# Two orders of work in a Hyena and retention block: retention beside the last input products, and beside the output projection

## The chip, the cores and the metric

The kernel runs on one core of a Trainium2 chip. The metric is the device time of one execution in microseconds; the time given is the median of several runs. The engines are PE (TensorE, matrix products), DVE (VectorE), ACT (ScalarE), POOL (GpSimd) and SP, which here only issues DMAs; "SP's queue" is the list of DMA issues that SP works off in program order, one wait after the other.

## The reference

One layer of a block with two kinds of token mixers that read the same projection of the normed and modulated input. T = D = 1024; the Hyena part has 512 channels, the retention part eight heads of 64, in chunks of 128 tokens, run in both directions.

```python
ux = hx @ w_in                                  # x0, x1, v of Hyena; q, k, v, g of retention
x0, x1, v = split(short_conv(u_hyena))
y_hy = bidir_long_conv(v * x1, filters, bias) * x0     # by FFT
q, k = rope(q), rope(k)                         # pairs of neighbouring channels are turned
o = retention(q, k, v, forward) + flip(retention(flipped, backward))
#   per chunk: (q k^T * decay mask) v  +  (q * w_q) state
o = (o - mean) * rsqrt(var + eps) * gn_g        # per head
y_ret = o * silu(g)
x = x + gate * (concat(y_hy, y_ret) @ w_out)
x = x + gate2 * relu(hx2 @ w1)^2 @ w2           # MLP, then a last norm
```

## The kernel before

All large products are made in three matmuls each (`mm3`, L182): an operand is split into a high part of reduced precision and a low rest, and high by high, high by low and low by high are added in PSUM. A weight is brought in as a *slab* of 256 or 512 columns: `slab` (L193) loads it in halves (`wr_...`), ScalarE casts the high part (`wh_...`), VectorE subtracts for the low part (`wl_...`). `prefetch` (L221) asks for the next slab of a fixed list (`order`). `hxh` and `hxl` are the input's two parts, feature by token.

The program is recorded in the order of the Python code and then ordered for each engine by a scheduler; work within `with urgent():` is given priority. What an engine, or a DMA queue, has in its list is worked off in that order.

The work in question runs in three stages.

*Convolution, about 256 to 511 us.* For each half `hv` of the 512 channels: products x1, vh and x0 (`feature_major`, tile `px...`), short convolutions on ScalarE and VectorE (`short_conv`, L818), a transform loop of eight rounds in which PE makes `pXv` (forward) and `pGv` (back) and VectorE multiplies by the filter and adds (`dft_const`, `butterflies`), and the gated result, stored as `mix_d` (tile `vxl`). Products of the next part stand between the rounds: those of x0 of the half, x1 and vh of the next, and in the second loop the gate products g (`pgt`, token by feature, `token_major`, L519). Among them stand the pieces of `modulation` (L686): eight loads of w_ada (`adaw`), eight VectorE operations that add them up (`adac`), four small products (`pada`). There are eight pieces in all; two of them stand in the second transform loop and behind it.

*q, 511 to 555 us.* q is made token by feature as well (`pq`, 384 matmuls of 256 columns; g has as many). `rope` (L551) turns it on VectorE (`qr`, `rpq`) and writes it twice side by side (`q`), so that `q_d` holds each head's 64 channels twice. Then the pools of the input parts are closed, and the places of the output projection opened (`big`, with `place`, L1012).

*Retention and output projection, 555 to 712 us.* The mixed Hyena channels are loaded back (`mraw`) and split into `mx` (`split_mix`, L1036). `retention` (L1059) is called for 16 chunks, eight of heads 0 to 3 and then eight of heads 4 to 7. For one chunk it loads q (`q2l`), k, v and the states (`ktl`, `vtl`, `stl`); PE transposes q of four heads (`pqd`, L1074); VectorE makes `qw` (q times the decay) and ScalarE copies q into tiles with zeros in the other head's rows (`sgqz`); two products of 256 columns make the scores (`psc`, L1083); VectorE multiplies them with the mask (`sT`); 16 small products of 64 columns, two side by side in PE's columns, make the output `po` (L1093); VectorE and ScalarE form mean and square sums (`mu`, `ctrs`, `sqo`, `gss`). After four chunks `group_norm` (L1105) scales, multiplies by silu(g), transposes (`pz`) and writes the two parts `mr`. With every second chunk stands one `out_conv` (L1045), 24 matmuls `poh` of 512 columns that multiply the mixed Hyena channels by half of w_out, added to x (`XN`). After that `out_ret` (L1228) does the same for `mr` (`por`, 192 matmuls), and the MLP follows, which takes the second half of the time.

PSUM: `ps_mm` gives tiles of two banks for the large products; `ps_aux` and `ps_cv` (L176, L179) give single banks, by two tags.

## Time and profile before

| | |
|---|---|
| median of 3 runs | 1372.75 us (1372.7 to 1382.48) |
| profiled execution | 1372.26 us |
| its span | 1370.5 us |
| mean granted PE clock | 0.979 of full |
| PE busy | 1284.9 us, 94% |
| VectorE busy | 964.2 us, 70% |
| ScalarE busy | 524.7 us, 38% |
| DMA traffic | 278.19 MB, mean 203 GB/s |

The profiled execution's own time holds 1.8 us around its span. All rows are of this one execution. A matmul row's duration overlaps with the next one's; the pace is the distance between starts. A time line's row gives the start, the duration, the engine, the line and the operation, and in brackets how long the engine had stood idle and what ended that. The granted clock is a share of full speed: 1.00 is 2.4 GHz, and 0.50 would be 1.2 GHz throughout.

### The profile page before, as it was taken

To read this page: it belongs to the slowest core of one execution; us is meant where nothing else is said; L and a number is where in the kernel's file an instruction comes from. 1 tells how busy PE (TensorE), PEld (TensorE's weight loads), DVE (VectorE), ACT (ScalarE), POOL (GpSimd) and SP (SyncE) were. 2 spreads that over 40 slices of the span, in tenths; PEclk is the share of its full clock that TensorE was granted. 3 is DMA by queue.
4 is the path that set the end of the run, shared out by engine and by line. 5 is a ranking of instruction groups with operands and counts; after the bars stand their busy time and mean duration, and the time that the engine had idled before them with its cause. 6 is when DMAs were issued, how large, how long until landed. Compare 5 with 4: busy or idle time off the path is not lost.

```text
span 1370.5 us, 20044 instructions
## 1 busy us (share of the span) xinstructions
PE 1284.9 (94%) x7374; PEld 1075.9 (79%) x7374; DVE 964.2 (70%) x1709; ACT 524.7 (38%) x903; POOL 19.9 (1%) x24
## 2 busy tenths in 40 slices
PE   6899899999998989799897999999998999999996
PEld 1488788878887989677776888887886888888896
DVE  5798587557788766558887988888656955555563
ACT  6654422222132121223455444444444744344420
POOL 0310000000000000000000000000000000000000
PEclk9899999999999999999998999999999999999999
DMA  9545656465436544875321788988636996666621
GB/s 372 212 154 162 215 177 194 143 204 170 139 133 202 178 155 169 274 241 182 114 87 60 251 299 326 337 311 292 245 123 227 342 321 187 196 200 186 198 79 62
DMA packets 139570, 278.19 MB, mean 203 GB/s; under 512 B 14672, under 2 KB 47056, under 8 KB 137040
## 3 DMA queue, kind: packets, MB, share of 16 engines
q1 hardware_dynamic: 137744, 272.19, 59.4%
q0 software_dynamic: 1152, 4.19, 0.8%
q8 instruction: 58, 0.95, 0.3%
q10 hardware_dynamic: 576, 0.52, 0.1%
q14 instruction: 40, 0.33, 0.1%
HBM read 193.75 MB, written 83.10 MB: 202 GB/s over the span
## 4 chain that ended last, share of the span: by engine, by line
PE 72%; DVE 11%; DMA 9%; ACT 4%; issue 3%; SPq 1%; POOL 0%; DVEq 0%; ACTq 0%; POOLq 0%
PE px L185 6%; PE px L183 5%; PE px L184 5%; PE py L185 5%; PE py L183 5%; PE py L184 5%; PE pw L183 4%; PE pw L185 4%; PE pw L184 4%; DMA dft_f_k<-in_dft_f 1%; PE pGv L886 1%; PE psc L1083 1%; PE pq L185 1%; PE pq L184 1%; PE pq L183 1%
## 5 line engine op out<-in xcount | busy, mean ns | idle before, releaser
L1176 DVE TENSOR_TENSOR mt<-tr,mt 128x512 fp32r<-128x512 f32 x112 | 76.8, 688 | 99.1 <-ACT mt L1175 98.8
L1175 ACT CAST mt<-tr 128x512 fp32r<-128x512 f32 x112 | 69.5, 621 | 123.6 <-PE py L185 65.2
L183 PE MATMUL px<-mt,mw 128*128 128x512 f32 (+1 forms) x320 | 112.0, 350 | 2.9 <-ACT mw L1175 2.3
L184 PE MATMUL px<-mt,mw 128*128 128x512 f32 (+1 forms) x320 | 112.2, 351 | 1.0 <-DVE mt L1176 1.0
L185 PE MATMUL px<-mt,mw 128*128 128x512 f32 (+1 forms) x320 | 111.5, 349 | 0.1
L1176 DVE TENSOR_TENSOR mw<-wr,mw 128x512 fp32r<-128x512 f32 x112 | 76.7, 687 | 4.4 <-ACT mw L1175 4.3
L183 PE MATMUL py<-mt,mw 128*128 128x512 f32 x192 | 74.7, 389 | 0.0
L184 PE MATMUL py<-mt,mw 128*128 128x512 f32 x192 | 74.7, 389 | 0.0
L185 PE MATMUL py<-mt,mw 128*128 128x512 f32 x192 | 74.7, 389 | 0.0
L1175 ACT CAST mw<-wr 128x512 fp32r<-128x512 f32 x112 | 69.0, 617 | 9.3 <-DMA wr<-s_d 4.8
L183 PEld LDWEIGHTS px<-mt,mw 128*128 128x128 f32 x320 | 60.9, 190 | 11.3 <-ACT mw L1175 2.8
L184 PEld LDWEIGHTS px<-mt,mw 128*128 128x128 f32 x320 | 60.9, 190 | 9.3 <-DVE mt L1176 1.3
L185 PEld LDWEIGHTS px<-mt,mw 128*128 128x128 f32 x320 | 60.8, 190 | 8.4 <-DVE mw L1176 0.7
L183 PE MATMUL px<-hxh,wh_x 128*128 128x512 f32 x128 | 50.9, 398 | 0.0
L185 PE MATMUL px<-hxh,wl_x 128*128 128x512 f32 x128 | 50.9, 398 | 0.0
L184 PE MATMUL px<-hxl,wh_x 128*128 128x512 f32 x128 | 50.7, 396 | 0.0
L697 DVE SCALAR_TENSOR_TENSOR adac<-adaw,cs,adac 128x512 f32<-128x512 f32 x56 | 41.9, 748 | 11.2 <-DMA adaw<-in_w_ada 10.4
L185 PE MATMUL pk<-wh_k,hxl 128*128 128x256 f32 x128 | 39.4, 307 | 3.1 <-DVE hxl L423 3.1
L184 PEld LDWEIGHTS py<-mt,mw 128*128 128x128 f32 x192 | 36.0, 188 | 7.5
L183 PEld LDWEIGHTS py<-mt,mw 128*128 128x128 f32 x192 | 36.0, 188 | 7.5
L185 PEld LDWEIGHTS py<-mt,mw 128*128 128x128 f32 x192 | 36.0, 188 | 7.4
L184 PE MATMUL pk<-wl_k,hxh 128*128 128x256 f32 x128 | 38.4, 300 | 0.9 <-DVE wl_k L207 0.9
(491 smaller groups left out, 3731.5 us busy)
## 6 DMA issues: line engine op xcount, KB each, us to landing
tr<-t_d SPq DMA_DIRECT2D x112, 256.0 KB, 4.0
adaw<-in_w_ada SPq DMA_DIRECT2D x64, 256.0 KB, 4.2
WH<-in_w_mlp SPq DMA_DIRECT2D x16, 1024.0 KB, 7.6
s_d<-WH SPq DMA_DIRECT2D x16, 1024.0 KB, 4.8
wr<-s_d SPq DMA_DIRECT2D x64, 256.0 KB, 4.0
wr<-in_w_mlp SPq DMA_DIRECT2D x48, 256.0 KB, 4.2
t_d<-c SPq DMA_DIRECT2D x40, 256.0 KB, 4.0
t_d<-CH SPq DMA_DIRECT2D x40, 256.0 KB, 5.0
```

The source lines that it names most:

```text
L183: PE.matmul(o, lhsT=lh, rhs=rh, start=first, stop=False, **kw)
L184: PE.matmul(o, lhsT=lh, rhs=rl, start=False, stop=False, **kw)
L185: PE.matmul(o, lhsT=ll, rhs=rh, start=False, stop=last, **kw)
L697: V.scalar_tensor_tensor(ac, wa, cs[:, k, 0:1], ac, op0=ALU.mult, op1=ALU.add)
L886: PE.matmul(o, lhsT=y[:, 0, cb], rhs=iv[:, sl[0]], start=True, stop=False)
L1083: PE.matmul(pc[:, pr * 256:(pr + 1) * 256], lhsT=kt[:, pr], rhs=qT[:, 2 * pr:2 * pr + 2].rearrange("p h c -> p (h c)"), start=True, stop=True)
L1175: A.copy(hi, src)
L1176: V.tensor_tensor(lo, src, hi.bitcast(F32), op=ALU.subtract)
```

## The change

*Columns of w_in.* The host reorders q's and k's columns of each head, so that a rope pair's first members stand in the first 32 channels and the second members in the other 32. `rope` (now for k alone) swaps halves instead of neighbours, and the form that writes its result twice is gone. A new constant `ropeT` holds the tables feature by token.

*Slabs.* Loads of the seventh slab and later ones are issued by GpSimd in place of SP. The list has x0's slabs behind x1 and vh of both halves, then q, g of heads 0 to 3 and q, g of heads 4 to 7.

*Convolution.* The loop over `hv` is cut into `conv_in`, `conv_gate`, `conv_dft` and `conv_out`, called in another order; the five modulations here stand after the first input part, after the second, and after the first gate part.

*q and g* are made feature by token. q0 and g0 come after the convolution's code, q1 and g1 in eight parts of 24 matmuls (`last_products`). `rotate` turns q: four DMAs swap the 32-row halves into `qs`, three VectorE operations of 128x1024 follow, and the result goes to `q_d`.

*Retention* loads q already transposed, each chunk twice (`q2`, upper and lower 64 rows). Transposes, zero tiles and copies go; the scores are four products of 64 rows and 128 columns into a `ps_cv` and a `ps_aux` bank; `sT` is made in two halves.

*Heads.* `heads(0)` runs the eight chunks of heads 0 to 3, with two parts of `last_products` ahead and one after each of the first six. The gate is multiplied in together with the norm's weight, and results go to DRAM (`y_d`). Then the pools are exchanged, and `heads(1)` runs the other eight chunks, with one `out_conv` after each; the earlier results are loaded back and split (`split_ret`). A pool `gap` keeps room so that `mx`, `mr00` and `mraw` lie where the first heads' tables do not.

```diff
-            SP.dma_start(raw, src[:, ks])
+            (SP if nxt[0] < 6 else G).dma_start(raw, src[:, ks])
...
+    yy0 = conv_dft(0, conv_in(0))
+    for _ in range(2):
+        modulation()
+    vT1 = conv_in(1)
+    for _ in range(2):
+        modulation()
+    conv_gate(0)
+    modulation()
+    with urgent():
+        conv_out(0, yy0)
+    conv_gate(1)
+    yy1 = conv_dft(1, vT1)
+    with urgent():
+        conv_out(1, yy1)
...
+    def rotate(hh, b, qf):
+
+        qs = scp.tile([P, T], F32, tag="sc", bufs=3, name=f"qs{hh}{b}")
+        for i in range(4):
+            SP.dma_start(qs[32 * i:32 * i + 32], qf[32 * (i ^ 1):32 * (i ^ 1) + 32])
+        V.tensor_tensor(qs, qs, rot[:, 1], op=ALU.mult)
+        V.tensor_tensor(qf, qf, rot[:, 0], op=ALU.mult)
+        V.tensor_tensor(qf, qf, qs, op=ALU.add)
+        SP.dma_start(q_d[hh][b * P:(b + 1) * P], qf)
+
+    def last_products():
+
+        for kind in "qg":
+            wh, wl = slabs.pop((kind, 1))
+            for b in range(2):
+                o = scp.tile([P, T], F32, tag="sc", bufs=3, name=f"{kind}f1{b}")
+                for h in range(2):
+                    ps = ps_cv(f"p{kind}1{b}{h}")
+                    cc = slice(512 * h, 512 * h + 512)
+                    for k in range(KC):
+                        mm3(ps, wh[:, k, b * P:(b + 1) * P], wl[:, k, b * P:(b + 1) * P], hxh[k][:, cc], hxl[k][:, cc],
+                            k == 0, k == KC - 1)
+                    with urgent():
+                        if kind == "q":
+                            A.copy(o[:, cc], ps)
+                            if h:
+                                rotate(1, b, o)
+                        else:
+                            A.activation(o[:, cc], ps, AF.Silu)
+                            SP.dma_start(sg_d[2 + b][:, cc], o[:, cc])
+                    yield
             prefetch()
...
+        q2 = rtl.tile([P, 4, P], F32, tag="q2", bufs=2, name=f"q2l{nm}")
+        for r in range(2):
+            SP.dma_start(q2[64 * r:64 * r + 64], q_d[hh].rearrange("(h d) t -> d h t", h=4)[:, :, n * P:(n + 1) * P])
...
-        pq = ps_aux(f"pqd{nm}")
-        for h in range(4):
-            PE.transpose(pq[:, h * P:(h + 1) * P], q2[:, h], ident)
...
-        pc = ps_aux(f"psc{nm}")
+        pc = ps_cv(f"psc{nm}0"), ps_aux(f"psc{nm}1")
         for pr in range(2):
-            PE.matmul(pc[:, pr * 256:(pr + 1) * 256], lhsT=kt[:, pr],
-                      rhs=qT[:, 2 * pr:2 * pr + 2].rearrange("p h c -> p (h c)"), start=True, stop=True)
+            for s in range(2):
+                rows = slice(64 * s, 64 * s + 64)
+                PE.matmul(pc[s][:, pr * P:(pr + 1) * P], lhsT=kt[rows, pr], rhs=q2[rows, 2 * pr + s],
+                          start=True, stop=True)
...
-        V.tensor_tensor(ctr, ctr, sg, op=ALU.mult)
...
-            hi, lo = mr[g][0][:, blk], mr[g][1][:, blk]
-            A.activation(hi, pt, AF.Copy, scale=gn)
-            V.scalar_tensor_tensor(lo, pt, gn, hi.bitcast(F32), op0=ALU.mult, op1=ALU.subtract)
+            V.scalar_tensor_tensor(sg[:, pr], pt, gn, sg[:, pr], op0=ALU.mult, op1=ALU.mult)
+            if hh == 0:
+                SP.dma_start(y_d[pr][g], sg[:, pr])
+            else:
+                split_ret(g, blk, sg[:, pr])
...
+    for _ in range(2):
+        next(products)
+
+    heads(0, last_heads)
...
+    for k in range(4):
+        split_mix(k)
+    for d in range(KC):
+        SP.dma_start(xn[d], I["xT"][d * P:(d + 1) * P])
...
+    heads(1, projection)
```

On VectorE, at the first chunk of heads 0 to 3, the order is now this; `qs` and `qf` are the two tiles of `rotate` for q1, `wl_g` is a slab's low part.

```order
L212 TENSOR_TENSOR wl_g_4730<-wr_g_4735,wh_g_4729 128x1024
L1012 TENSOR_TENSOR qs_4806<-qs_4806,rot 128x1024
L1013 TENSOR_TENSOR qf_4753<-qf_4753,rot 128x1024
L1084 TENSOR_TENSOR qw_0_4826<-q2l_0_4816,tabq_4751 128x512
L1014 TENSOR_TENSOR qf_4753<-qf_4753,qs_4806 128x1024
L1094 TENSOR_TENSOR sT_0_4834<-psc_00_4828,tabq_4751 128x2x128
L1094 TENSOR_TENSOR sT_0_4834<-psc_01_4829,tabq_4751 128x2x128
```

Before, `qw` and `sT` of the first chunk stood among the low parts of `mx`, behind the rope of the last q products; now rotate's three operations stand ahead of `sT`.

On PE, a late chunk of heads 0 to 3 stood like this before (`po` rows are those of one chunk, the number behind a name tells buffers apart):

```order
L1083 MATMUL psc_7_5902<-sgqz,ktl_7_5886 128x256 x2
L1074 MATMUL pqd_0_5966<-cols,q2l_0_5957 128x128 x4
L183 MATMUL poh_6340<-mx_5398,wh_o_5557 128x512
L184 MATMUL poh_6340<-mx_5399,wh_o_5557 128x512
L185 MATMUL poh_6340<-mx_5398,wl_o_5558 128x512
L1093 MATMUL po_7_5907<-vtl_7_5888,sT_7_5905 64x64 x2
L1093 MATMUL po_7_5907<-stl_7_5890,qw_7_5898 64x64 x2
```

and the second chunk of these heads stands like this now, where `pq` is a matmul of a product part:

```order
L190 MATMUL pq_4861<-hxh_348,wl_q_4616 128x512
L1090 MATMUL psc_10_4899<-q2l_1_4887,ktl_1_4890 128x128
L1090 MATMUL psc_11_4900<-q2l_1_4887,ktl_1_4890 128x128
L1090 MATMUL psc_10_4899<-q2l_1_4887,ktl_1_4890 128x128
L1090 MATMUL psc_11_4900<-q2l_1_4887,ktl_1_4890 128x128
L1090 MATMUL psc_21_4981<-q2l_2_4968,ktl_2_4971 128x128 x2
L1102 MATMUL po_1_4908<-vtl_1_4892,sT_1_4905 64x64 x2
L1102 MATMUL po_1_4908<-stl_1_4894,qw_1_4897 64x64 x2
L188 MATMUL pq_4933<-hxh_341,wh_q_4615 128x512
L1102 MATMUL po_1_4908<-vtl_1_4892,sT_1_4905 64x64 x2
```

The transposes are gone, the scores are single products by turns into two banks with half of the next chunk's behind them, and products no longer stand between scores and `po`.

On SP, where q's products ended and the mixed channels were loaded, the queue before was:

```order
L994 DMA q_d_4391<-q_5239 128x2x512
L994 DMA q_d_4391<-q_5247 128x2x512
L1021 DMA tabq<-tab_d 128x2048
L1040 DMA mraw<-mix_d_2891 128x512
L994 DMA q_d_4391<-q_5352 128x2x512
L1040 DMA mraw<-mix_d_2891 128x512
L1040 DMA mraw<-mix_d_2892 128x512
L205 DMA wr_o_5563<-in_w_out 128x1024
L994 DMA q_d_4391<-q_5360 128x2x512
```

and between the first and the second four heads it is now:

```order
L1224 DMA XN_5425<-in_xT 128x1024 x4
L1129 DMA y_d_1_4490<-sgs_4750 128x512
L1129 DMA y_d_1_4492<-sgs_4750 128x512
L1075 DMA q2l_0_5483<-q_d_4488 64x4x128 x2
L1077 DMA ktl_0_5486<-kT_d_1345 128x256
L1062 DMA tabq<-tab_d 128x2048
L1197 DMA mraw<-mix_d_2891 128x512 x2
L1197 DMA mraw<-mix_d_2892 128x512 x2
```

The loads `mraw<-mix_d` stood behind stores of q; now they stand behind the stores `y_d` of the last group norm of heads 0 to 3, behind q and k of the next chunk and behind a table.

## Rows read from the trace of the kernel before

**Rows 1.** The page: busy us, share of the span, instructions.

```profile
PE 1284.9 (94%) x7374; PEld 1075.9 (79%) x7374; DVE 964.2 (70%) x1709; ACT 524.7 (38%) x903; POOL 19.9 (1%) x24
```

**Rows 2.** Stretches: seconds; busy us (instructions) of five engines; granted PE clock; DMA share; GB/s.

```profile
380.00:405.00 25.00, 25.00 (x115) 20.62 (x114) 20.76 (x38) 7.58 (x11) 0.00 (x0) 1.00 0.31 115
500.00:525.00 25.00, 21.53 (x175) 21.32 (x174) 9.46 (x14) 5.08 (x6) 0.00 (x0) 0.93 0.48 167
525.00:550.00 25.00, 25.00 (x223) 25.00 (x222) 16.45 (x24) 2.11 (x2) 0.00 (x0) 1.00 0.42 153
550.00:575.00 25.00, 17.14 (x86) 13.24 (x85) 13.95 (x21) 7.76 (x12) 0.00 (x0) 0.86 0.77 245
```

**Rows 3.** Time line of PE, one chunk: start, us, instruction, count, [idle before].

```profile
630.91 0.34 PE L1093 MATMUL po<-vtl,sT 128*64 128x64 f32 x4
...
631.99 0.50 PE L185 MATMUL poh<-mx,wl_o 128*128 128x512 f32 x1
...
632.80 1.02 PE L1083 MATMUL psc<-sgqz,ktl 128*128 128x256 f32 x4
633.66 0.60 PE L1074 MATMUL pqd<-cols,q2l 128*128 128x128 f32 x4
634.01 0.47 PE L185 MATMUL poh<-mx,wl_o 128*128 128x512 f32 x1
```

**Rows 4.** Time lines of PE and VectorE, second convolution half.

```profile
441.16 0.67 PE L886 MATMUL pGv<-dft_i_v,yv 128*128 128x256 f32 x2 [3.30 <-issue]
...
502.66 0.75 DVE L697 SCALAR_TENSOR_TENSOR adac<-adaw,cs,adac 128x512 f32<-128x512 f32 x1 [3.75 <-DMA adaw<-in_w_ada]
...
506.15 1.05 PE L700 MATMUL pada<-ones,adac 128*128 128x2 f32 x8 [3.47 <-DVE adac L697]
```

**Rows 5.** Time line of all engines, from q's products to out_conv.

```profile
556.87 0.50 PE L183 MATMUL poh<-mx,wh_o 128*128 128x512 f32 x1 [2.04 <-ACT mx L1042]
557.87 0.37 SPq L994 DMA_DIRECT2D q_d<-q  x1
...
558.28 1.22 SPq L1040 DMA_DIRECT2D mraw<-mix_d  x2
...
559.73 0.77 PE L183 MATMUL poh<-mx,wh_o 128*128 128x512 f32 x1 [2.36 <-DVE rpq L558]
...
562.10 1.21 ACT L1042 CAST mx<-mraw 128x512 fp32r<-128x512 f32 x2 [5.29 <-DMA mraw<-mix_d]
...
562.51 0.80 PE L184 MATMUL poh<-mx,wh_o 128*128 128x512 f32 x1 [2.01 <-DVE mx L1043]
```

**Rows 6.** Time line of PE, a chunk of heads 0 to 3.

```profile
610.91 1.13 PE L1083 MATMUL psc<-sgqz,ktl 128*128 128x256 f32 x4 [1.88 <-ACT sgqz L1080]
```

**Rows 7.** Time line of PE, out_ret.

```profile
678.66 0.80 PE L183 MATMUL por<-mr,o3h 128*128 128x512 f32 x1 [2.79 <-DVE XN L1243]
679.25 0.63 PE L184 MATMUL por<-mr,o3h 128*128 128x512 f32 x1
...
684.80 0.41 PE L185 MATMUL por<-mr,o3l 128*128 128x512 f32 x1
```

**Rows 8.** Groups of VectorE (busy us, mean ns), then time lines: last po, last scaled ctrs.

```profile
L1086 DVE TENSOR_TENSOR sT<-psc,tabq 128x512 f32<-128x512 f32 x16 | 11.0, 689 | 4.1 <-PE psc L1083 3.8
...
L564 DVE TENSOR_TENSOR q<-qr,rpq 128x1024 f32<-128x1024 f32 x2 | 2.4, 1190 | 0.0
...
661.54 0.29 PE L1093 MATMUL po<-stl,qw 128*64 128x64 f32 x4
...
665.13 1.22 DVE L1112 TENSOR_TENSOR ctrs<-ctrs,rso 128x1024 f32<-128x1024 f32 x1
```

**Rows 9.** DMA issues, 500 to 712 us: count, KB each, median us to landing.

```profile
q2l<-q_d SPq DMA_DIRECT2D x16, 256.0 KB, 3.2
XN<-in_xT SPq DMA_DIRECT2D x8, 512.0 KB, 7.4
...
mraw<-mix_d SPq DMA_DIRECT2D x8, 256.0 KB, 5.9
```

More of the change, by code (lines that the diff above doesn't have):

```diff
@@ L824, in short_conv, with conv_in @@
                                op0=ALU.mult, op1=ALU.add)
-    for hv in range(2):
+    def conv_in(hv):
         vT = vtp.tile([P, NCH, 256], F32, tag="vT", name=f"vT{hv}")
-        Gs = cvp.tile([P, 2, 8, 256], F32, tag="Gs", name=f"Gs{hv}")
         x1t = []
@@ L999, in tile_hymba_block, with last_heads @@
+    opool("gap", side="right").tile([P, 4 * 1024], F32, name="gap")
+    open_retention()
+    retention_tables(lambda nm: rt["l" if nm == "tabq" else "p"].tile([P, 4, 512], F32, name=f"{nm}0"))
+    products = last_products()
+    def last_heads(g, j):
+        next(products, None)
+    for _ in range(2):
+        next(products)
+    heads(0, last_heads)
+    cpool("rtp")
+    cpool("rtl")
+    cpool("gap")
     cpool("vtp")
```

284 lines of the change are left out of this document (150 added, 134 removed).

## The prediction

> **What bounds the kernel now.** I read the busy times first: PE works 94% of the span [rows 1], so a microsecond is gained only where PE has less to do, stands idle, or runs at the lower of its two clocks. Next the table of stretches, for those three. The products run at their pace where the clock is granted in full: 115 matmuls of 512 columns in 25 us, 0.217 us each, and 223 of 256 columns in 25 us, 0.112 us each [rows 2]. Twice the second is the first, so products written feature-major (384 of 512 columns in place of 768 of 256) gain nothing. In the stretches of 500 and 550 us PE lacks time and clock (0.93 and 0.86) [rows 2]. Then the time lines there, for what PE waited for. Three places stand out.
>
> - The second convolution half: 3.30 us ahead of a pGv, and 3.47 us ahead of a pada, where VectorE's adac had itself waited 3.75 us for a load of w_ada [rows 4].
> - The step from q's products to the out_conv products: 2.04, 2.36 and 2.01 us [rows 5]. On SP the store of q stands at 557.87, and the mraw loads go out behind it at 558.28; their data are there at 562.10, when ScalarE casts them. A load that needs nothing waited because the store ahead of it in the queue did.
> - The last out_ret products: 2.79 us, then matmuls at 0.427 us (13 steps from 679.25 to 684.80), the lower clock [rows 7].
>
> **What the change removes.** I sum against the profiled execution's 1372.26 us; the median of the runs, 1372.75, is 0.5 above it, and I make nothing of that.
>
> - Transposes: four take 0.35 us (633.66 to 634.01) [rows 3], in 16 chunks: -5.6. The wait of 1.88 us for ScalarE's copy of them [rows 6]: -1.9.
> - Scores: two products took 0.86 us (632.80 to 633.66) [rows 3], recorded as four matmuls of 256 columns, 0.215 each. Now there are four products of 128 columns on half the rows each, taken by turns from the upper and the lower 64 rows into two banks: the same 0.86 if they run one behind the other, 0.43 if pairs run side by side. The trace has no row-split matmul, but po is split by columns: 32 entries of 64 columns in 1.08 us (630.91 to 631.99) [rows 3], 0.034 each, where 64/256 of 0.215 is 0.054, so those pairs gain a factor of 1.6. I take that, 0.54: -5.1, with -6.9 and 0 as bounds.
> - The step at 555 to 572: 6.4 us of waits, and 0.14 of 25 us in clock, 3.5 [rows 2, 5]: -9.9. What is late there instead stands below.
> - out_ret: 2.79, and 5.55 us for 13 matmuls that cost 2.8 at full pace [rows 7]: -5.5. The group norm that made VectorE late there no longer multiplies by the gate in an extra pass, and its products are ready earlier.
> - Convolution: no modulation stands in the second loop now. Its two waits are 6.8 us, and the clock loses 0.07 of 25 us at the one [rows 2, 4], which I assume at the other too: 10.3. The pada wait must go (5.2); the other was for a chain on VectorE in which adac was only a part, so I take -9 in all. Bounds: -10.3, and +3.5 if the modulations, which now stand among the short convolutions and the first loop, bring one such wait more than they take.
>
> Sum: -37.0.
>
> The slab loads from the seventh on, issued by GpSimd, I cost at nothing: each is asked for one product part ahead, some 5 us of PE. If that cover fails, a part waits for the rest of its load: at XN's 7.4 us for as many bytes [rows 9], 2.2, in up to four parts 9. It belongs to the range. rope loses no operation. The changed order of convolution parts keeps products beside every step of the first DFT loop.
>
> **What it adds.** (1) *Ahead of the first scores.* After the second q product part PE has only the scores and then the first po, which needs sT. On VectorE sT stands behind rotate's three operations of 128x1024, the first of which waits for four moves of q's halves, which wait for ScalarE's copy. Copy 0.6 (two casts of 128x512 take 1.21) [rows 5]; the moves, which no row shows, as q2l's 3.2 [rows 9]; three operations at 1.19, as q's add [rows 8], 3.6; qw 0.7 and half of sT 0.35 [rows 8]: 8.4, less the scores' 0.5: 7.9. After such a wait PE ran at half clock [rows 7], which cost 2.7. Together +10.6; bounds 4 (the moves in 2, no clock lost) and 13.
>
> (2) *The chunks of heads 0 to 3.* The scores write two banks that the product parts also use, so a part stands behind po, not between scores and po. Per chunk PE waits for both halves of sT, 0.69 [rows 8], and I add 0.4 for two hand-overs: 1.1, in seven chunks +7.7. Bounds: 0.4 each, where the next scores already ran ahead (3), and 1.9 each, as the wait of this kind [rows 6] (13).
>
> (3) *From the first to the second four heads.* SP's queue has the two y_d stores of the last group norm, then q2l, ktl, tabq and only then the mraw loads, which wait for nothing else; and all out_conv products need mx from mraw. From the last po to the scaled ctrs the same chain takes 661.83 to 666.35, 4.5 us [rows 8]; the transposes (0.9, as many columns as the scores had) and two operations of the size of sT, 1.4: 2.3. Then five issues at some 0.4 (0.37 for a store) [rows 5], 2.0; a mraw load, 3.8 in the first of these rows [rows 5] and 5.9 in the median [rows 9], taken as 4.8; the cast 0.6; and VectorE's lo halves of the first two, as sT, 1.4. That is 15.6, less 1.3 for transposes and scores in between: 14.3, plus the half clock's 2.7: +17.0; bounds 11 and 24.
>
> (4) *Heads 4 to 7.* Five or more out_conv products stand between scores and po, over 1 us, so that (2) doesn't recur; with out_ret +1, bounds 0 and 5.5.
>
> Sum: +36.3. In all 1372.26 - 37.0 + 36.3 = 1371.6.
>
> The trace's price for changing between whole and split use of PE's array is in these rows: po's 1.08 us hold 0.1 us more than its eight groups at 0.12, and that is all a change and the way back can have cost. The Trainium skill (TensorEngine Tiling (Array Packing), Tiling Modes) speaks against the new scores: changing the tiling mode, not just the tile, drains the engine. With two changes more in each chunk at 0.1, 16 chunks would cost 3.2 us, and the sum would be 1374.8.
>
> **The rivals.**
> *The new waits come out at their low ends.* The same places, but the moves land in 2 us, scores run ahead in every chunk, and the clock is given back at once. Then (1) is 4, (2) 3, (3) 14.3 without the clock: -6.6, -4.7, -2.7, and the full convolution gain -1.3: 1356.3. For it: the order of PE has half of the next chunk's scores ahead of some po. Against it: around the long waits of rows 5 and 7 the clock did fall.
> *SP's queue becomes the bound: slower.* The loads of chunks 4 to 7 stand behind sg_d and q stores that wait for product parts, and 4 MB of XN loads (eight) go out just ahead of the y_d stores. XN loads land in 7.4 us, mraw in 5.9 [rows 9]. If loads behind waiting stores take 7.4, they are longer than a product part (24 x 0.217 = 5.2): 2.2 more in each of four chunks, 8.8, and at (3) 2.6 for mraw plus 7.4 for XN in its way, 10: 1390.4. It decides from the point at which such a load takes longer than one part. For it: exactly this queue held mraw before. Against it: the chunks' own loads land in some 3 us [rows 9], well within a part.
> *The row-split scores run one behind the other.* +5.1: 1376.7. For it: no row shows them; against it: po. It lies within the forecast's band.
>
> **How the numbers follow.** The forecast, with the third rival in it, gets 0.44, the first rival 0.32, the slow one 0.24. 1% is 13.7 us, about what a measurement of this kernel can tell from no change: faster is below 1359, slower above 1386.5. The first rival lies beyond the one, the second beyond the other. Terms (1) to (3) are sums of gaps that no row shows; their bounds reach 17 below and 15 above, and with those of scores, convolution and (4) 21 below: 1350. Upward the slow rival lies past them, at 1390. So the range is 1350 to 1390, and the forecast's own, with half of these bounds, 1361 to 1380.
>
> **What would show it.** Right: no pqd; out_ret without a gap; no pada in the second DFT loop and the clock full there; after the second pq part of heads 4 to 7 a wait of about 8 us for sT; about 1 us ahead of po in each early chunk; and one stretch without PE of 12 to 16 us between the last pz of the first heads and the first poh, with mraw issued just behind y_d. Scores of 0.54 per chunk. Wrong: mraw landed before the group norm ended; waits of one kind that recur in each chunk above 2 us; or the convolution no shorter.

## The result, and the profile after

The changed kernel takes 1396.27 us in the median of four runs (1393.23 to 1405.89), beside 1374.64 us of the kernel before in four runs on the same chip: a ratio of 1.0148, with an interval of 1.0113 to 1.0183. It is slower by about 1.5%; 1371.6 was forecast, and the time lies above the range as well. The profiled execution took 1393.23 us with a span of 1391.4, against 1372.26 and 1370.5.

The page's busy line answers to [rows 1]:

```profile
PE 1285.0 (92%) x6990; PEld 1056.5 (76%) x6990; DVE 961.1 (69%) x1707; ACT 520.2 (37%) x881; POOL 30.5 (2%) x44
```

PE is busy for the same 1285 us, in a span that is 20.9 us longer. To see where these went I cut both spans at ends and starts of PE's work that both kernels have: the last `ps` (which ends the first stage), the last `pgt` (half of the q and g products done, the convolution behind it) and the first `py` (the MLP).

| stretch | before | after | difference | forecast |
|---|---|---|---|---|
| start, up to the last `ps` | 255.7 | 262.0 | +6.3 | 0 |
| convolution and half of q and g | 255.6 | 247.9 | -7.7 | -9 |
| rest of q and g, heads, output projection | 200.8 | 222.1 | +21.3 | +8.3 |
| MLP, to PE's last instruction | 652.2 | 652.5 | +0.3 | 0 |

The heads are the place. The stretches of the changed kernel there (columns as in [rows 2]) show two holes:

```profile
500.00:525.00 25.00, 20.96 (x92) 16.88 (x90) 12.41 (x22) 5.58 (x8) 1.06 (x2) 1.00 0.69 227
525.00:550.00 25.00, 15.45 (x115) 12.09 (x116) 9.25 (x16) 1.30 (x3) 0.00 (x0) 0.66 0.64 174
550.00:575.00 25.00, 22.28 (x167) 17.58 (x167) 12.73 (x22) 7.41 (x11) 1.05 (x2) 0.93 0.55 168
575.00:600.00 25.00, 18.65 (x196) 14.98 (x195) 12.48 (x29) 3.81 (x7) 0.53 (x1) 1.00 0.63 203
600.00:625.00 25.00, 8.51 (x33) 6.23 (x34) 9.39 (x16) 5.92 (x9) 0.00 (x0) 0.52 0.73 260
```

Between 600 and 625 us PE works for 8.5 us of 25, at a granted clock of 0.52; between 525 and 550 us it works at 0.66. PE's time line of the changed kernel has these waits:

```profile
531.80 1.22 PE L1090 MATMUL psc<-q2l,ktl 64*128 64x128 f32 x8 [10.85 <-DMA ktl<-kT_d]
535.62 0.48 PE L1102 MATMUL po<-vtl,sT 128*64 128x64 f32 x4 [2.60 <-issue]
...
555.31 0.34 PE L1102 MATMUL po<-vtl,sT 128*64 128x64 f32 x4 [0.50 <-DVE sT L1094]
...
564.97 0.34 PE L1102 MATMUL po<-vtl,sT 128*64 128x64 f32 x4 [2.15 <-issue]
...
607.14 1.97 PE L1124 MATMUL pz<-cols,ctrs 128*128 128x128 f32 x8 [11.08 <-DVE ctrs L1120]
614.52 1.22 PE L1090 MATMUL psc<-q2l,ktl 64*128 64x128 f32 x8 [5.41 <-DMA ktl<-kT_d]
619.68 1.22 PE L188 MATMUL poh<-mx,wh_o 128*128 128x512 f32 x2 [3.93 <-ACT mx L1199]
...
630.79 0.72 PE L1090 MATMUL psc<-q2l,ktl 64*128 64x128 f32 x8
631.44 0.50 PE L190 MATMUL poh<-mx,wl_o 128*128 128x512 f32 x1
...
721.06 0.50 PE L188 MATMUL por<-mr,o3h 128*128 128x512 f32 x1 [0.45 <-DVE XN L1341]
```

The first two rows are the waits ahead of the first scores and of the first `po`, the next two smaller ones in later chunks, and then come three waits in a row at the step to heads 4 to 7. The scores' rows answer to [rows 3]: 0.65 us from their start to that of the next product. The last is all that is left of the gap of out_ret [rows 7].

What PE waited for at the step stands on ScalarE and VectorE. ScalarE first:

```profile
597.08 0.42 ACT L1109 ACTIVATE sqo<-ctrs 128x256 f32<-128x256 f32 x1 [1.39 <-DVE ctrs L1106]
602.35 1.04 ACT L211 CAST wh_o<-wr_o 128x1024 fp32r<-128x1024 f32 x1 [4.84 <-DMA wr_o<-in_w_out]
603.41 1.28 ACT L291 ACT_TABLE_LOAD   x1
604.70 0.22 ACT L291 ACTIVATE rs_yo<-gss 128x16 f32<-128x16 f32 x1
```

The cast of the last half of the last slab stands ahead of the group norm's `rs_yo` and waits 4.84 us for its load, which GpSimd issued at 593.98. VectorE shows the same order, with `wl_o` ahead of the norm:

```profile
597.99 0.17 DVE L1116 TENSOR_SCALAR gss<-gss 128x16 f32<-128x16 f32 x1
603.42 1.23 DVE L212 TENSOR_TENSOR wl_o<-wr_o,wh_o 128x1024 fp32r<-128x1024 f32 x1 [5.26 <-ACT wh_o L211]
604.95 0.25 DVE L292 RECIPROCAL rs_yo<-rs_yo 128x16 f32<-128x16 f32 x1 [0.30 <-ACT rs_yo L291]
...
605.86 1.23 DVE L1120 TENSOR_TENSOR ctrs<-ctrs,rso 128x1024 f32<-128x1024 f32 x1
```

At the start VectorE's rotate waits for its moves:

```profile
531.09 1.23 DVE L1012 TENSOR_TENSOR qs<-qs,rot 128x1024 f32<-128x1024 f32 x1 [11.21 <-DMA qs<-qf]
...
535.10 0.75 DVE L1094 TENSOR_TENSOR sT<-psc,tabq 128x256 f32<-128x256 f32 x2
```

SP's queue has what was due before both places:

```profile
517.85 0.92 SPq L977 DMA_DIRECT2D mix_d<-vxl  x2
...
521.60 2.58 SPq L1011 DMA_DIRECT2D qs<-qf  x4
524.23 0.63 SPq L1075 DMA_DIRECT2D q2l<-q_d  x1
524.90 0.60 SPq L1077 DMA_DIRECT2D ktl<-kT_d  x1
...
609.08 1.18 SPq L1129 DMA_DIRECT2D y_d<-sgs  x2
...
612.74 2.38 SPq L1197 DMA_DIRECT2D mraw<-mix_d  x4
```

And the DMA issues from 500 to 732 us (count, KB each, median us to landing) answer to [rows 9]:

```profile
XN<-in_xT SPq DMA_DIRECT2D x8, 512.0 KB, 8.7
...
wr_o<-in_w_out POOLq DMA_DIRECT2D x4, 512.0 KB, 7.1
...
mraw<-mix_d SPq DMA_DIRECT2D x8, 256.0 KB, 5.0
...
qs<-qf SPq DMA_DIRECT2D x8, 128.0 KB, 6.4
```

The moves take 6.4 us in the median of all eight, where the prediction had 3.2. The four that the first chunk waits for land 7.4 to 7.9 us after their issue, and from the first issue to VectorE's first operation 9.5 us pass (521.60 to 531.09). The first chunk's own k, `ktl`, issued at 524.90, takes 6.8 us, and the first scores wait for it.

### The profile page after: what moved, and what is told of

It is laid out like the page before. It is cut to its first block, busy times and chain, and to the rows that moved or that the text cites. A ratio compares the mean times of both kernels' runs of the same rounds, so it can differ in the third digit from the quotient of the medians.

```text
span 1391.4 us, 19304 instructions
## 1 busy us (share of the span) xinstructions
PE 1285.0 (92%) x6990; PEld 1056.5 (76%) x6990; DVE 961.1 (69%) x1707; ACT 520.2 (37%) x881; POOL 30.5 (2%) x44
## 4 chain that ended last, share of the span: by engine, by line
PE 74%; DMA 9%; DVE 6%; issue 3%; ACT 2%; SPq 1%; ACTq 0%; DVEq 0%; POOLq 0%
PE px L189 6%; PE px L190 6%; PE px L188 6%; PE py L188 5%; PE py L189 5%; PE py L190 5%; PE pw L188 5%; PE pw L189 5%; PE pw L190 5%; DMA wr_o<-in_w_out 1%; DMA dft_f_k<-in_dft_f 1%; PE poh L188 1%; PE poh L189 1%; PE poh L190 1%; PE pq L188 1%
```

## The experiments

All but three are the changed kernel with one edit or several. "Heads" below is the third stretch of the table: 222.1 us in the changed kernel, 200.8 before. Letters in the expectations stand for causes: A is the slab half's cast ahead of the group norm at the step, D rotate ahead of the first chunk's masks, D' late loads for the first chunk. Ratios are to the kernel before, run on the same chip in the same sitting; medians of different kernels can be from different chips. Of the single edits only the first gives an interval clear of the changed kernel's (1.0113 to 1.0183): what the others are worth is read from the waits of one profile each.

### Slab loads back on SP

```diff
-            (SP if nxt[0] < 6 else G).dma_start(raw, src[:, ks])
+            SP.dma_start(raw, src[:, ks])
```

> All slab loads are issued by SP again. Question 1, the start: before the convolution the changed kernel is 5 to 8 us later in every run so far, from about 42 us on, where a VectorE operation waits 1.7 us instead of 1.0 for a store that GpSimd issues (eo_d) and PE then falls to half clock. If it is the use of GpSimd's queue for more loads, that wait is 1.0 again and the convolution begins at about 256 us instead of 260 to 264; if it is anything else of the change (another constant in memory), it stays at 1.7 and 260 to 264. Question 2, between the heads: theory A (a slab half ahead of the group norm) expects no gain, since the half still waits for the one raw buffer and stands on SP ahead of XN or behind it: from the last po to the scaled ctrs 8 us or more.

Measured: 1383.56 us in eight runs, ratio 1.0068 (1.0047 to 1.0088), heads 213.7. This one line is worth about 11 us: the median lies 10.7 us above that of the kernel before on the same chip, where the changed kernel's lay 21.6 above. In the profiles 8.4 us of it are in the heads. Its DMA issues:

```profile
wr_o<-in_w_out SPq DMA_DIRECT2D x4, 512.0 KB, 4.6
...
qs<-qf SPq DMA_DIRECT2D x8, 128.0 KB, 2.3
```

the first moves and VectorE's operation behind them:

```profile
522.49 2.42 SPq L1011 DMA_DIRECT2D qs<-qf  x4
...
526.73 1.23 DVE L1012 TENSOR_TENSOR qs<-qs,rot 128x1024 f32<-128x1024 f32 x1 [6.79 <-DMA qs<-qf]
```

and PE's time line:

```profile
528.92 1.23 PE L1090 MATMUL psc<-q2l,ktl 64*128 64x128 f32 x8 [7.08 <-DMA ktl<-kT_d]
531.26 0.48 PE L1102 MATMUL po<-vtl,sT 128*64 128x64 f32 x4 [1.12 <-issue]
...
596.06 1.97 PE L1124 MATMUL pz<-cols,ctrs 128*128 128x128 f32 x8 [7.34 <-DVE ctrs L1120]
609.04 0.80 PE L188 MATMUL poh<-mx,wh_o 128*128 128x512 f32 x1 [11.01 <-ACT mx L1199]
```

The moves fall from 6.4 to 2.3 us in the median, those of the first chunk from 9.5 to 4.2 between first issue and first operation, its `ktl` from 6.8 to 2.5, and the halves of the last slabs from 7.1 to 4.6. The wait ahead of the first `po` is 7.08 + 1.12 = 8.2 us instead of 13.45, and the 2.15 of a later chunk is gone too. At the step the waits only change places: the norm's by 3.7 us less, but then `mraw`, now behind an XN load as well, keeps PE for 11.01. The expectation's first question is answered too: the start stays late (264.1 us, the wait for the store 1.76), so that it is not the slab loads on GpSimd's queue that delay it. Its second missed narrowly: from the last `po` to the scaled `ctrs` it is 7.3 us, not 8 or more.

The line reaches further than the heads. In the nine profiles with slab loads on GpSimd the convolution stretch takes 246.3 to 252.5 us, in the mean 249.7; in the six with them on SP (this one and the five of "The causes together") 243.2 to 246.8, in the mean 244.6. What is faster there was not followed up. The slab loads are not: the 14 halves that go out between 270 and 514 us land in 4.0 us in the median when GpSimd issues them, and in 4.1 from SP.

### The last slab's cast out of the group norm's way

First only the call that asks for the slab was moved:

```diff
                     yield
-            prefetch()
+            if kind == "q":
+                prefetch()
...
         out_conv(4 * g + j)
+        if (g, j) == (0, 0):
+            prefetch()
```

> The second w_out slab is asked for in the first chunk of heads 4 to 7 instead of behind the last input products; nothing else changes. Theory A (the group norm of heads 0 to 3 was late because ScalarE's cast and VectorE's subtraction of that slab's second half, whose load landed 8 us after its issue, stood ahead of it): from the last po to the scaled ctrs 11.0 us become about 4.5, and the whole time falls by about 6.5. Rival B (the SP queue behind the y_d stores, and the 4 MB of XN loads, set the start of the second heads): the group norm is early, but the first scores and poh then wait that much longer for ktl and mraw; the time falls by less than 2.

Measured: 1393.1 us, ratio 1.012 (1.0045 to 1.0195); the norm's wait is 11.12 us as before the edit. The slab's work is urgent, and the scheduler put it where it had been, on every engine: no test of the theory, but a repeat, whose heads of 219.1 say that such a stretch scatters by some 3 us from one profile to another. So the slab was written out behind `mx`, through `mraw`'s places:

```diff
         out_conv(4 * g + j)
+        if (g, j) == (0, 0):
+            o1 = [wpool.tile([P, 4, 512], F32R, tag=t, bufs=2, name=f"{t}_o1") for t in ("wh", "wl")]
+            slabs["o", 1] = o1
+            for a in range(2):
+                hi, lo, raw = [t[:, 2 * a:2 * a + 2] for t in (*o1, mraw)]
+                SP.dma_start(raw, I["w_out"][1][:, 2 * a:2 * a + 2])
+                A.copy(hi, raw)
+                V.tensor_tensor(lo, raw, hi.bitcast(F32), op=ALU.subtract)
```

> What the first trial could not move: the second w_out slab is now loaded through mraw, behind the mixed channels, so that its casts can't stand ahead of the group norm. Theory A: from the last po to the scaled ctrs 11.0 us become 4.5, and the time falls by about 6.5. Rival B (the loads set the start): the scores then wait for ktl and the poh for mraw as much longer, since 4 MB of XN are still landing; the time falls by less than 2.

Measured: 1391.06 us in two runs, ratio 1.0132 (1.0053 to 1.0211), heads 216.7. PE's time line at the step:

```profile
604.49 1.97 PE L1125 MATMUL pz<-cols,ctrs 128*128 128x128 f32 x8 [5.19 <-DVE ctrs L1121]
611.53 1.23 PE L1091 MATMUL psc<-q2l,ktl 64*128 64x128 f32 x8 [5.08 <-DMA ktl<-kT_d]
617.27 1.22 PE L188 MATMUL poh<-mx,wh_o 128*128 128x512 f32 x2 [4.51 <-ACT mx L1200]
```

The first of the three waits falls from 11.08 to 5.19 and the others stay: the slab's half was 5.9 us of it, and 5.2 is the norm's own chain, near the 4.5 that [rows 8] gave. That is close to theory A's 6.5; the longer waits behind it that rival B expected did not come.

### The stores y_d and the loads behind them

`y_d` on GpSimd's queue alone (`SP.dma_start(y_d...)` becomes `G.dma_start`):

> The y_d stores are issued by GpSimd's queue instead of SP's, so that q2l, ktl, tabq and mraw no longer stand behind them. Theory B (the order of SP's queue): the 5.4 us ahead of the first scores of heads 4 and 3.9 us ahead of the first poh go, about -9. Theory A (the group norm's chain and the slab ahead of it): the 11.1 us ahead of pz stay as they are, and the gain of the two waits is there only as far as scores or poh may run before; their order stays pz, scores, poh, so -9 holds for both in the waits behind pz and none in front of it. Rival C (the loads are slow because 4 MB of XN are under way, not because they were issued late): less than -3.

Measured: 1393.29 us, ratio 1.0122 (1.0057 to 1.0186), heads 215.0. The norm's wait is still 11.18, but the scores' behind it falls from 5.41 to 0.50 us: q and k no longer stand behind `y_d`. In the third place 2.50 us are left of 3.93. The 9 us of theory B are not reached in these waits (6.2), and `ktl`, issued at 602.92, lands only 10.6 us later, while the 4 MB of XN are landing. With this, the slab behind `mx` and each XN load beside its own product:

```diff
-    for d in range(KC):
-        SP.dma_start(xn[d], I["xT"][d * P:(d + 1) * P])
...
+        SP.dma_start(xn[4 * g + j], I["xT"][(4 * g + j) * P:(4 * g + j + 1) * P])
         out_conv(4 * g + j)
```

> The second w_out slab behind the mixed channels, the y_d stores on GpSimd's queue, and each XN load with the out_conv that needs it, instead of 4 MB at once ahead of mraw. If the three queues (ScalarE's cast, SP's stores, XN) are together the whole of the 22 us without products between the last po of heads 0 to 3 and the first poh, that stretch becomes 6 to 8 us (the group norm's chain, 4.5, and one cast and subtraction), with no half clock behind it: -15 to -18 in the whole time. If something else holds it (the exchange of the pools, the tables), more than 12 us are left.

Measured: 1391.47 us from two runs 14 us apart, ratio 1.0135 (0.9989 to 1.028); in the profile, taken of the longer one, heads of 219.2 and waits of 4.50 and 9.51 us at the step. The expectation was missed: the scheduler put `mraw` behind two XN loads, k and the table in SP's queue. Moving calls in the text changed the order of the queue in ways that were not asked for.

### How many product parts stand ahead of the first scores

`range(2)` becomes `range(1)`, or `range(4)`, in the loop that calls `next(products)`.

> One product part ahead of the first scores instead of two, so that rotate's first call comes after the first chunk. Theory D (rotate ahead of sT, and its four moves ahead of k and v in SP's queue, made the start): the 10.85 and 2.60 us of waits and some 3 us of half clock become about 1.1: -15 in the whole time, as long as the later parts cover the same chunks. Rival: the first chunk waits for its own loads anyway (q2l and tabq go out only some 2 us before), and the wait stands one part earlier: less than -4.

> Four product parts ahead of the first scores instead of two. With one part PE stood idle for 12.4 us until nearly the same moment, so theory D' is: the first chunk's loads, on SP behind the last mix_d stores and the moves of rotate, are there at about 532 us, and whatever products PE has until then are free cover. Two more parts are 11 us: the wait ahead of the first scores falls from 10.85 to under 2, the po behind it may keep 1 to 2.6, the half clock goes (3), and the last four chunks, now without products, cost 1 to 1.5 us each for sT: -8 to -12 in all. Rival: rotate's second and third call shift onto the first scores in turn, and the wait moves with the parts: less than -3.

Measured with one: 1397.39 us, ratio 1.0151 (1.0076 to 1.0226), heads 220.6. PE's row:

```profile
531.96 1.22 PE L1090 MATMUL psc<-q2l,ktl 64*128 64x128 f32 x8 [12.41 <-DMA ktl<-kT_d]
```

The scores start at the same moment as with two parts, 531.96 against 531.80, though the queue no longer has rotate's moves ahead of them, as the rival said: the loads go out behind the last stores `mix_d` in any case. `ktl` goes out 1.5 us earlier, at 523.41, and takes 8.4 us instead of 6.8. The moves alone are thus not what makes it late; with the slabs on SP it took 2.5. At the step the waits changed places again: 5.28 us for the norm, 13.77 for `mx`.

With four: 1386.78 us, ratio 1.0101 (1.002 to 1.0181), heads 213.2, and 1.01 + 1.28 + 2.25 = 4.5 us of waits at the start instead of 13.45: the parts cover the late loads. Not all of the gain is theirs. The last slab is now asked for earlier, its last half is cast at 583.60, long ahead of the norm, and the norm's wait is 5.29 us instead of 11.08. Against that, chunks that have no product part any more wait for `ktl` and `ctrs` (2.22 and 1.11 us).

### Rotate's calls behind the chunk

```diff
                             if h:
-                                rotate(1, b, o)
+                                turns.append((1, b, o))
...
         next(products, None)
+        if turns:
+            with urgent():
+                rotate(*turns.pop(0))
```

> The changed kernel with rotate's two calls for q1 behind the first and the second chunk instead of ahead of the first. Theory D (rotate on VectorE ahead of sT, its moves on SP ahead of k and v): of the 10.85 and 2.60 us at the start of the first heads 7 or more go, and some of the half clock; -8 to -11. Theory D' (the loads of the first chunk go out only behind the last mix_d stores and are slow): the 10.85 shrink by 3 at most, the 2.60 go, since sT no longer stands behind three operations: -4 to -6.

Measured: 1391.64 us, ratio 1.0133 (1.0087 to 1.0179), heads 218.4. PE's time line:

```profile
528.17 1.23 PE L1092 MATMUL psc<-q2l,ktl 64*128 64x128 f32 x8 [6.82 <-DMA ktl<-kT_d]
530.33 0.48 PE L1104 MATMUL po<-vtl,sT 128*64 128x64 f32 x4 [0.93 <-DMA vtl<-v_d]
```

The first two waits fall from 10.85 and 2.60 to 6.82 and 0.93; one of 3.02 comes in the third chunk, and the 2.15 of the fourth falls to 0.55. So of 13.45 us ahead of the first `po` about 5.7 go with rotate and its moves, and 7.75 are left for loads that are late without them: between what theory D and theory D' say.

### The order of the row halves in the scores

```diff
-        for pr in range(2):
-            for s in range(2):
+        for s in range(2):
+            for pr in range(2):
```

> The four score products of a chunk in another order: first the two of the upper 64 rows, then the two of the lower, so that neighbours no longer stand in different halves of the rows. If products of different halves run side by side, a chunk's scores, 0.65 to 0.72 us where the clock is full, become about 0.86 or more, +2 to +3 us in the whole time; if they don't, they stay at 0.65 to 0.72 and the time doesn't move.

Measured: 1398.61 us, ratio 1.016 (1.0053 to 1.0267), heads 222.9. A chunk's scores in PE's time line:

```profile
630.78 0.72 PE L1090 MATMUL psc<-q2l,ktl 64*128 64x128 f32 x8
631.43 0.51 PE L190 MATMUL poh<-mx,wl_o 128*128 128x512 f32 x1
```

They cost 0.65 us in either order: taking the upper and lower rows by turns brings nothing. The expectation took this for a sign that the halves run one behind the other, but the records say otherwise: in both orders the eight records of a chunk start two by two, 0.01 us apart, at 0, 0.21, 0.33 and 0.44 us. Where four records of one half stand alone (573.87 to 574.20 in the changed kernel) they start one by one, 0.11 apart. So a pair takes the time of one, and the order of the halves does not matter for that.

### The causes together

Slabs on SP, four parts and the last slab behind `mx`; then with the mixed channels' loads on GpSimd's queue, which has no more to do; then with `y_d` there too; then `y_d` by ScalarE instead; then rotate's calls behind the chunk as well:

```diff
-            SP.dma_start(raw, mix_d[k][:, cc])
+            G.dma_start(raw, mix_d[k][:, cc])
...
-                SP.dma_start(y_d[pr][g], sg[:, pr])
+                A.dma_start(y_d[pr][g], sg[:, pr])
```

> Three single edits of earlier runs together: slab loads on SP, four product parts ahead of the first scores, second w_out slab behind the mixed channels. If what they free is separate, the part from the end of the g products to the MLP, 222 us in the changed kernel and 213.7, 213.2 and 216.7 in the three, becomes 222 - 8.4 - 8.9 - 5.4 = 199; but the first and the third both took time from the group norm's wait (11.1 to 7.3 and to 5.2), and the first two from the start (13.4 to 8.2 and to 4.5), so I expect 203 to 207, and 1374 to 1379 in all. More than 210 would say that the waits are of one cause that moves on.

> The kernel of the three edits, and the mixed channels' loads on GpSimd's queue, which is empty then, instead of SP's behind the y_d stores. By the theory of SP's queue the first poh no longer wait for mx, only the scores for ktl: of the 9 to 11 us behind the group norm's transposes 4 or more go. If the loads are slow because of the XN loads under way, they land no earlier: less than -2.

> The same, and the y_d stores on GpSimd's queue too, so that the first chunk's q, k, v of heads 4 to 7 are asked for before the group norm ends. What is left of the stretch between the heads is the group norm's chain, 4.5 to 5 us, and one cast and subtraction, 1.3: 6 to 8 us without products; another -4 to -5 against the run with the mixed channels alone, if SP's order is the cause.

> The run with the mixed channels on GpSimd, and the y_d stores issued by ScalarE, so that neither SP's loads nor the mixed channels' stand behind them. By the theory of SP's queue the scores no longer wait for ktl (8.4 us there): the stretch between the heads is the group norm's chain, about 5, and 1 to 2 more: -6 to -8 against the run with the mixed channels alone, 1370 to 1373 in all. If the 4 MB of XN hold the loads, 4 us or more of the wait stay.

> The last kernel with rotate's calls for q1 behind the first and second chunk as well. With four parts ahead and no rotate ahead of sT the start of the first heads waits 1.5 us or less where 3.6 and 3.5 were: -6 to -9 against the last kernel, 1362 to 1367 in all, and faster than the kernel before by 5 or more.

| kernel | runs | median us | ratio (interval) | heads |
|---|---|---|---|---|
| three edits | 7 | 1381.26 | 1.0078 (1.0043 to 1.0114) | 212.2 |
| and `mraw` by GpSimd | 10 | 1378.08 | 1.0048 (1.0017 to 1.008) | 210.7 |
| and `y_d` by GpSimd | 6 | 1380.85 | 1.008 (1.0043 to 1.0117) | 210.0 |
| `y_d` by ScalarE instead | 8 | 1375.41 | 1.0003 (0.9971 to 1.0036) | 208.9 |
| and rotate behind the chunk | 10 | 1377.57 | 1.0027 (0.9996 to 1.0058) | 207.6 |

The three edits gave 8.4, 8.9 and 5.4 us of the heads alone, and together only 9.9, less than the 15 to 19 that were expected: they shared the same waits, the norm's above all. With four parts and slabs on SP the first `po` still waits 3.63 us, a later one 3.58, and the step 5.27 + 5.23 + 3.64. The queue changes then move waits about. With `mraw` by GpSimd the 3.64 for `mx` go and the scores' wait grows to 8.38. With `y_d` there too the first `mraw` loads, which had gone out at 493.67, stand behind it and go out at 596.58, and PE waits 4.76 us for them; the 4 to 5 us expected of this edit did not come. From row to row the heads move by less than such a stretch scatters; of the ratios, the fourth kernel's stands clear of the first's and the third's. In the fourth kernel PE's waits at the step are

```profile
592.33 1.94 PE L1125 MATMUL pz<-cols,ctrs 128*128 128x128 f32 x8 [5.28 <-DVE ctrs L1121]
598.34 1.23 PE L1091 MATMUL psc<-q2l,ktl 64*128 64x128 f32 x8 [4.07 <-DMA ktl<-kT_d]
```

and the first `mraw` loads go out long ahead of the step, in GpSimd's queue, and `ktl` ahead of the `y_d` stores, which ScalarE issues at 594.24:

```profile
494.01 2.23 POOL L1198 DMA_DIRECT2D mraw<-mix_d  x4 [400.88 <-DVE ibbfa L913]
...
592.17 0.33 SPq L1078 DMA_DIRECT2D ktl<-kT_d  x1
```

Its expectation named what would speak for XN: 4 us or more of the scores' wait left. 4.07 are left. No `y_d` store stands ahead of `ktl` any more, and yet it takes 6.0 us, while the XN loads land (the last at 596.94); in the changed kernel, where they had all landed, it took 2.8. That the traffic of XN slows the loads beside it fits this and the 10.6 us above, but no run took XN away alone.

This kernel takes the time of the kernel before: what was lost in the medians is recovered by where transfers are issued, by two more product parts ahead of the first scores, and by a norm with nothing ahead of it. Its heads are 8.1 us longer than before, near the 8.3 that was forecast for the change. None goes below the kernel before. The last edit was to do that, and missed: the two waits at the start are gone (3.64 and 3.46 us), but one of 3.19 comes in a later chunk, and at the step the scores' wait is 5.42.

### Parts of the change in the kernel before

Three kernels start from the one before: with the table `ropeT` as an unread constant; with that and the new order of q's and k's columns with its `rope`; and with the convolution's new order alone.

> The kernel before with one thing of the change: the new constant ropeT stands among its inputs and is not read. If the 5 to 8 us that the changed kernel loses ahead of the convolution come from where things lie in memory, its eo_d wait becomes 1.7 us instead of 1.0, PE falls to half clock from about 42 us on and the convolution begins 5 to 8 us later: +5 to +8. If they come from code or from chance, it starts at 256 us and measures as the kernel before.

> The kernel before with the first part of the change alone: q's and k's columns reordered on the host, halves swapped in rope instead of neighbours, ropeT among the inputs and not read. If this part costs the 4 to 9 us that all kernels of the changed family lose ahead of the convolution, it begins at 260 or later; if not, at about 255.5, as in the kernel before with ropeT alone, and +0 to +3 in all.

> The kernel before with the convolution in the change's order alone (first DFT, second half's first two products, both gates, the output of each half by rows of its own tag, five modulations inside it); gate and query products, their layout, and the retention are those of the kernel before. Theory (the convolution's new order is the gain the prediction costed at 9, and everything lost lies behind it): from the end of the modulated shift product to the end of the gate products 255.6 goes to 244 to 250, the heads stay at 200.8 within 3, the start at 255.7 or up to 6 more, as the kernels with the same code there scattered; time 1362 to 1370, ratio 0.991 to 0.997. Rival (the modulations, which the change also moved out of the gate products into the convolution, were what filled the gate products' waits; or the gain came from the query and gate products that follow): the stretch stays within 3 of 255.6 and the time within 0.3% of before.

| kernel | runs | median us | ratio (interval) | start | convolution | heads |
|---|---|---|---|---|---|---|
| unread `ropeT` | 10 | 1375.26 | 1.0035 (1.0002 to 1.0067) | 256.1 | 251.3 | 202.7 |
| and columns, `rope` | 8 | 1375.99 | 1.0001 (0.9978 to 1.0025) | 261.6 | 252.5 | 201.6 |
| convolution's order | 12 | 1373.66 | 0.9993 (0.9966 to 1.002) | 262.3 | 249.2 | 200.5 |

The start's +6.3 us needs none of the change: the kernel with the convolution's order has the code of before there and takes as long as the changed one, and so does the second, which has the new `rope` of k in this stretch. Up to 240 us all 19 kernels profiled here have the same operations in the same order on every engine. VectorE's time line of the second shows the first difference, ahead of any `rope`:

```profile
41.40 0.69 DVE L444 TENSOR_TENSOR eo<-peo,dec 128x512 f32<-128x512 f32 x1 [1.64 <-DMA eo_d<-eo]
```

where the kernel before waited 1.02 us for the same store. From 40 to 60 us the granted clock was 0.83 in the kernel before and 0.57 in this one, and the start of the k products moves from 51.3 to 56.8. By this clock the 19 profiles fall into two groups: in five it is 0.83 to 0.88, and the stretch ends at 255.7 to 259.6 us; in fourteen it is 0.55 to 0.66, and the stretch ends at 260.4 to 265.5. Each group has kernels with the code of before and changed ones. What draws the one or the other was not found: the late store at this place alone isn't it, since in four of the fourteen VectorE waits only 0.23 or 0.24 us there. In the group of the higher clock the kernels with the code of before end at 255.7 and 256.1 and the changed ones at 259.1 to 259.6, so that some 3 us may belong to the change; that too stays open.

The convolution's order brought no time, though the stretch and the heads came out as expected. Its stretch of 249.2 us stands below all three profiles of the old order (255.6, 251.3, 252.5), but only 3.9 below their mean, and the median is the same. Waits in it on PE add up to 4.1 us here, and to 6.3, 8.1 and 10.7 in those three.

## Why the prediction was wrong

*Removed.* Transposes, the wait for the zero tiles' copies, the step at 555 us and the gap of out_ret went as the prediction said; PE waits 0.45 us in out_ret where it lost 5.5 [rows 7]. Scores: 0.65 a chunk, not 0.54, so -3.4 instead of -5.1. Convolution: -7.7 for -9 in this pair of profiles, but the sum was made against the longest of three profiles of the old order, and the order alone shortened the stretch by 3.9 against their mean and the time by nothing that was measured. In the six changed kernels with slab loads on SP the stretch is in the mean 8.5 below that mean (244.6 for 253.1): there the 9 comes near, and slab loads on GpSimd took about 5 of it.

*(1) The start, +10.6.* Waits of 13.45 us, and the clock of 0.66 behind them: 23 `pq` took 7.17 us there and 5.47 in other stretches, and the whole is near 17. The step that failed is "The slab loads from the seventh on, issued by GpSimd, I cost at nothing", with its bound of 9. The prediction asked only whether a slab would come in time, and not what it does to transfers of SP that run beside it. From the first issue to the first operation the moves take 9.5 us with the slab loads on GpSimd and 4.2 with them on SP, where 3.2 was taken; and the first chunk's k, for which nothing was taken, takes 6.8 and 2.5. With this line undone the wait is 8.2, and 7.9 was worked out. This line is also the largest single cause that the times show: about 11 us of 21.6. The Trainium skill (DMA: Bandwidth & Descriptors, Latency and other measured facts) puts the first byte of a GpSimd-issued transfer at about 1 us and of an SP-issued one at about 0.6; for the same 512 KB the trace's difference is larger in the heads, 2.5 us, and none in the convolution (4.0 and 4.1). Its rule that the two kinds feed different queues inside a DMA engine, which takes them by turns (SWDGE vs HWDGE vs iDMA), would let a slab slow the moves; no run here shows that mechanism.

*(2) The chunks, +7.7.* The waits of the later chunks add up to 5.2 us, with 1.45 of lower clock 6.7. The sum is right, in part by luck: about 1.1 was forecast for each chunk, and most have 0 to 0.55, while one `po` alone waits 2.15, behind the half of a slab on VectorE, and has the lower clock behind it.

*(3) The step, +17.0.* The three waits are 20.4 us and the lower clock some 3.6: 24, the bound. The step that failed is "From the last po to the scaled ctrs the same chain takes 661.83 to 666.35, 4.5 us": the chain was taken from a place where nothing else stood in the queues of ScalarE and VectorE. Here both had the last slab's half ahead of the norm, and it took 11.0 us, of which the run with the slab behind `mx` gave back 5.9. The queue behind it, y_d stores ahead of q, k, table and `mraw`, stood as forecast, but took 9.9 us from the first store to the first cast (609.08 to 619.01) where 6.8 was taken: 3.7 for the issues instead of 2.0, and 6.3 for the first `mraw` load instead of 4.8. It is made up in part by a first `poh` that starts 0.7 us behind that cast, where 2.0 was taken, and by 3.2 us of transposes and scores in between, where 1.3 was.

*(4) Heads 4 to 7.* +0.45 for +1. Right.

*The sum.* In the heads (1) to (4) come to 17 + 6.7 + 24 + 0.4 = 48 instead of 36.3, which is 11.8 more, and the scores to 1.7 more: 13.5. Measured against forecast, the heads are 21.3 - 8.3 = 13.0 longer. What is left of the 20.9 is the start's 6.3, which the kernel with the convolution's order, with the old code there, has as well, against the convolution.

*The range.* Its upper end was drawn short of the prediction's own bounds. Downward it adds those of (1) to (3), of scores, convolution and (4), 21 in all; upward it adds only (1) to (3), 15, and takes the slow rival for the rest. The 9 of the slab loads, of which it says that "It belongs to the range", would have put the end at 1395, and with the scores' 5 it would be 1400, above the 1396.27 that was measured.

*The rivals.* The slow one came nearest in time (1390.4) and had the place right, SP's queue with XN and y_d ahead of `mraw`; but its price lay on the loads of chunks 4 to 7, and these were in time; the late ones were those of the first chunk. The third, scores one behind the other, came half true. On the scores the Trainium skill's rule (TensorEngine Tiling (Array Packing), Tiling Modes), that changing the mode drains the engine, fits: the eight records that start in pairs, with the next product at 0.65, make 0.43 as for pairs side by side and 0.1 at either end. That pairs run side by side with both orders of the halves was not expected, and no run took the change of mode alone.

## What to carry to other kernels

A transfer moved to another queue is not free because it comes in time itself: look at what else is in flight then, and at what a short transfer on the path takes beside it. A chain's length taken from one place holds elsewhere only if the in-order lists of its engines are empty there; before using it, list what stands between its instructions in the new order, loads' casts above all. Where several waits of one stretch have different causes, removing one uncovers the next, and a difference of a few us between two profiles is worth nothing until a second profile of the same code shows how far it scatters.

## What was not expected of the hardware

- Moves of 128 KB that SP issued while a 512 KB load issued by GpSimd was under way took 7.4 to 7.9 us, and 2.2 to 2.4 when SP had issued that load too; a 128 KB load of k beside them took 6.8 and 2.5. The load itself took 9.0 and 4.3 us there, but in the convolution, in the median of 14, 4.0 and 4.1.
- The granted clock between 40 and 60 us was either 0.83 to 0.88 or 0.55 to 0.66, with the same order of work on every engine, and the work up to the convolution ended at 255.7 to 259.6 us with the one and at 260.4 to 265.5 with the other.
- Four products of 64 rows and 128 columns take 0.65 us, whatever the order of the halves: records of the two halves start in pairs 0.11 us apart, and those of one half alone one by one at the same distance.
